# Feed-forward in steps of 512 hidden features, with block products of the next step between down products

## The chip, the cores and the metric

The kernel runs on one core of one Trainium2 chip. The metric is the device time in microseconds of one execution. The median of three runs of the kernel before is 1529.01 us (1528.41 to 1530.18). "The profile" is what the hardware profiler recorded in one execution; the engines are called PE (TensorE, matmuls), DVE (VectorE), ACT (ScalarE) and SP (SyncE, which issues the loads here).

## The reference

Two layers on a sequence of 16 + 512 positions of width 1024. Each has a token mixer and then a feed-forward part; only the latter is touched:

```python
def _sq_relu_mlp(h, w1, w2):
    return jnp.square(jax.nn.relu(h @ w1)) @ w2
...
        h = _layer_norm(DEEPNORM_ALPHA * h + _sq_relu_mlp(h, ffn_w1[layer], ffn_w2[layer]),
                        ln_g[layer, 1], ln_b[layer, 1])
```

`w1` is 1024 x 4096 and `w2` 4096 x 1024, in float32. Layer 0 works on all 528 positions (two halves of 264), layer 1 on the 512 that are returned (two halves of 256).

## The kernel before

**Precision.** Every operand of a product is split into a high part in the fast float32 format (an ACT cast, L228 for weights, which writes `wh`) and the remainder (a DVE subtraction, L229, which writes `wl`). A product runs three passes per 128 rows of the contraction: high by high, high by low, low by high. So the third matmul of a product is the first that needs `wl`.

**Weights.** `weight_plan` lists the weight tiles in the order of use. SP loads each into one of three `raw` buffers (`rpool`) of 128 x 1024 numbers. `weights(kind)` hands out the next item and prepares one or two items ahead. An item "A" is 1024 rows by 128 columns, an item "C" 512 rows by 256 columns, each one tile; an item "Q" is two tiles, for a block product. All split weights, activations and intermediates lie in 43 buffers of one pool (`upool`).

**Hidden features.** Feature tiles of 128: 32 of them in `ffn_w1`. The first eight are computed as plain products over K = 1024 (`job`, `squared`), six of them in `mlp_start`. The other 24 are computed two at a time as a **block product** (`quad_up`): the 1024 x 256 block of `w1` against both halves of the positions is formed with seven multiplications of half blocks in place of eight, in the manner of Strassen and Winograd. PE runs the seven in the order 11, a, b, 12, d, c, 22 (`multiply`), each 12 matmuls of half the positions. Their results go into the PSUM tiles `qa`, `qb`, `qc`, `qd`; the combinations are small DVE operations (L1167, L1169, L1174, L1176, L1180). 22 is left over (`finish`) and is run by `between` a little later; behind it come the squared ReLU (L1182), ACT's cast of g (L1183) and its remainder (L1184).

The weights of a block product need sums of blocks before they can be split. `quad_steps` is a generator, and each `advance()` runs one step of the next item that is not finished:

```python
        h, l = halves(r0)
...
        dve.tensor_tensor(out=s0.rearrange("p (a b) -> p a b", a=2), in0=r0.rearrange("p (a b) -> p a b", a=2),
                          in1=dup(r1[:, hi], 512), op=ALU.add)
...
        h, l = halves(s0)
        quad["c"], quad["a"] = (h[:, lo], l[:, lo]), (h[:, hi], l[:, hi])
...
        dve.tensor_tensor(out=s1[:, hi], in0=s1[:, lo], in1=r1[:, lo], op=ALU.add)
...
        h, l = halves(s1)
        quad["b"], quad["d"] = (h[:, lo], l[:, lo]), (h[:, hi], l[:, hi])
```

On DVE a preparation is thus L229 (first raw tile), L242 (first sums), L229 (first sums, for a and c), L248 and L250 (second sums), L253 (remainder of block 12), L229 (second sums, for b and d). ACT has the four casts.

**Down products.** The features of a group of eight tiles (`NG` = 4 groups) are multiplied with `w2`, one product over K = 1024 for each of the eight output tiles `y`; DVE adds each into `y` (L1096 the first time, L1094 later). In layer 0 such a product is 48 matmuls of 264 columns into `mm` (two PSUM buffers, shared with `qb` and `qd`), in layer 1 it is 24 matmuls of 512 columns into `bank` (four buffers, shared with `qa` and `qc`).

**The order.** Group 0's features, group 0's down products with two `advance()` behind each, then all four block products of group 1 and the first of group 2 in a row, group 1's down products, and so on. The last group goes to `tail`, which runs two products in full and the last six output tiles half by half, the layer norm between them. The compiler's scheduler puts the instructions of DVE, ACT and SP into an order of its own; with `pe.on` the order of the matmuls is held as written. Each engine then has a fixed list.

## Time and profile before

| | |
|---|---|
| median of three runs | 1529.01 us |
| the profiled execution | 1526.21 us |
| its span, first to last instruction | 1524.4 us |
| mean granted PE clock | 0.994 |
| DVE, additions of down products (L1094), layer 0 | 17 of 0.701 us, without the last group's half products |
| loads of raw tiles | 224 of 512 KB |

The span is the time from the first to the last instruction; the rest of the execution, 1.8 us, lies around it. "Busy" is the time in which an engine had an instruction running; matmuls overlap, so that one of 264 columns lasts 0.28 us but the next starts 0.12 us after it. Feed-forward 0 runs from about 345 to 725 us of the span, feed-forward 1 from about 1150 us to the end.

### The profile page before, as it was taken

Reading aid. Unit: us, or ns where it says so; the run is one execution under the profiler, and the core shown is the slowest. Engines: PE = TensorE matmul, PEld = TensorE weight load, DVE = VectorE, ACT = ScalarE, POOL = GpSimd, SP = SyncE. Lnnn points to the kernel's source line nnn. Section 1 sums busy time; section 2 is a strip of 40 time slices with the busy share of each in tenths; the row PEclk is TensorE's granted clock in tenths of the full one; section 3 lists DMA queues with packets and bytes.
Section 4 is the critical chain, followed back from the end, with each engine's and each line's share of the span. In section 5 each row is a group of like instructions: output and inputs, shape, how many; then the busy total and the mean of one; then the engine's idle time right before and its main releaser. Section 6 shows DMA issues by size and latency. Waiting matters only on the chain.

```text
span 1524.4 us, 23188 instructions
## 1 busy us (share of the span) xinstructions
PE 1485.1 (97%) x9752; PEld 1334.4 (88%) x9752; DVE 922.8 (61%) x1522; ACT 609.4 (40%) x972; POOL 0.2 (0%) x4
## 2 busy tenths in 40 slices
PE   8999999999999999999999999999999999999997
PEld 6887878799999999999888888888899888898986
DVE  4574466677758576568534354254477848676567
ACT  4474444536324233245343442153445524233323
POOL 0000000000000000000000000000000000000000
PEclk9999999999999999999999999999999999999999
DMA  6111102141313323243014035022150313313221
GB/s 243 51 48 55 56 29 85 57 138 32 97 55 91 116 70 125 71 132 117 28 42 137 14 109 166 0 89 90 56 168 27 111 56 97 124 62 133 83 70 56
DMA packets 39593, 129.02 MB, mean 85 GB/s; under 512 B 4725, under 2 KB 7173, under 8 KB 39489
## 3 DMA queue, kind: packets, MB, share of 16 engines
q1 hardware_dynamic: 39488, 127.54, 26.1%
q8 instruction: 76, 1.25, 0.3%
q14 instruction: 29, 0.23, 0.0%
HBM read 125.43 MB, written 2.10 MB: 84 GB/s over the span
## 4 chain that ended last, share of the span: by engine, by line
PE 86%; DVE 9%; ACT 2%; DMA 2%; issue 1%; ACTq 0%; DVEq 0%
PE bank L156 33%; PE mm L156 21%; PE v_ps L156 10%; PE qc L156 5%; PE o_ps L156 5%; PE s_ps L156 4%; DVE wl L229 3%; PE qa L156 3%; DMA raw<-in_w 2%; PE qd L156 2%; ACT wh L228 1%; PE t_ps L159 1%; PE qb L156 1%; PE sum_ps L156 1%; DVE up L1182 1%
## 5 line engine op out<-in xcount | busy, mean ns | idle before, releaser
L229 DVE TENSOR_TENSOR wl<-raw,wh 128x1024 fp32r<-128x1024 f32 x200 | 242.3, 1221 | 71.6 <-ACT wh L228 70.9
L228 ACT CAST wh<-raw 128x1024 fp32r<-128x1024 f32 x200 | 205.9, 1046 | 107.7 <-DMA raw<-in_w 75.8
L156 PE MATMUL bank<-g,wh 128*128 128x512 f32 (+2 forms) x800 | 202.3, 344 | 3.4 <-ACT g L1183 2.9
L156 PEld LDWEIGHTS bank<-g,wh 128*128 128x128 f32 x800 | 138.4, 190 | 22.0 <-ACT g L1183 3.1
L156 PE MATMUL bank<-hh,wh 128*128 128x512 f32 (+3 forms) x448 | 144.2, 337 | 0.0
L156 PE MATMUL bank<-hh,wl 128*128 128x512 f32 (+3 forms) x448 | 140.4, 330 | 0.0
L156 PE MATMUL mm<-g,wh 128*128 128x264 f32 x832 | 136.5, 286 | 2.5 <-ACT g L1183 2.0
L156 PE MATMUL bank<-g,wl 128*128 128x512 f32 (+2 forms) x400 | 136.5, 342 | 0.0
L156 PE MATMUL bank<-hl,wh 128*128 128x512 f32 (+3 forms) x448 | 120.8, 331 | 4.3 <-DVE hl L948 4.3
L156 PEld LDWEIGHTS mm<-g,wh 128*128 128x128 f32 x832 | 116.3, 190 | 2.9 <-ACT g L1183 2.2
L156 PE MATMUL qc<-tc,wh 128*128 128x264 f32 (+1 forms) x576 | 107.1, 284 | 2.0 <-ACT wh L228 1.8
L156 PEld LDWEIGHTS bank<-hh,wh 128*128 128x128 f32 x448 | 84.0, 188 | 10.7 <-ACT hh L960 1.2
L156 PE MATMUL mm<-s,wh 128*128 128x264 f32 x544 | 92.8, 292 | 0.5 <-DVE s L362 0.5
L156 PEld LDWEIGHTS qc<-tc,wh 128*128 128x128 f32 x576 | 89.0, 188 | 3.6 <-ACT wh L228 3.3
L156 PEld LDWEIGHTS bank<-hh,wl 128*128 128x128 f32 x448 | 83.9, 188 | 8.4
L156 PE MATMUL qc<-tc,wl 128*128 128x264 f32 (+1 forms) x288 | 82.5, 287 | 5.3 <-DVE wl L229 5.1
L156 PE MATMUL mm<-g,wl 128*128 128x264 f32 x416 | 85.0, 286 | 0.0
L156 PEld LDWEIGHTS bank<-hl,wh 128*128 128x128 f32 x448 | 72.6, 188 | 14.0 <-DVE hl L948 4.9
L156 PEld LDWEIGHTS bank<-g,wl 128*128 128x128 f32 x400 | 75.5, 189 | 9.3
L228 ACT CAST wh<-sums 128x1024 fp32r<-128x1024 f32 x48 | 50.4, 1049 | 76.8 <-DVE sums L242 32.5
L156 PEld LDWEIGHTS mm<-s,wh 128*128 128x128 f32 x544 | 74.9, 188 | 6.8 <-issue 2.3
L229 DVE TENSOR_TENSOR wl<-sums,wh 128x1024 fp32r<-128x1024 f32 x48 | 58.6, 1221 | 27.6 <-PE mm L156 10.3
(314 smaller groups left out, 3098.5 us busy)
## 6 DMA issues: line engine op xcount, KB each, us to landing
raw<-in_w SPq DMA_DIRECT2D x224, 512.0 KB, 4.1
xf<-in_x SPq DMA_DIRECT2D x8, 264.0 KB, 5.4
y<-in_x SPq DMA_DIRECT2D x8, 264.0 KB, 4.1
out<-y SPq DMA_DIRECT2D x8, 256.0 KB, 2.2
nb<-in_c_nb SPq DMA_DIRECT2D x4, 264.0 KB
rd<-in_c_rd SPq DMA_DIRECT2D x4, 256.0 KB
rd<-in_c_rm SPq DMA_DIRECT2D x4, 192.0 KB, 4.2
fm<-in_c_fm SPq DMA_DIRECT2D x1, 264.0 KB, 2.7
```

Source lines behind the costliest of these rows:

```text
L156: return self.put(nc.tensor.matmul(*a, **k))
L159: return self.put(nc.tensor.transpose(*a, **k))
L228: act.copy(out=wh, in_=raw)
L229: dve.tensor_tensor(out=wl, in0=raw, in1=f(wh), op=ALU.subtract)
L1182: dve.scalar_tensor_tensor(out=rs, in0=rs, scalar=0.0, in1=rs, op0=ALU.max, op1=ALU.mult)
```

## The change

The hidden features are taken in steps of 512 (four feature tiles, two block products) in place of groups of 1024. The down product of a step is over K = 512, with C tiles of `w2`: one C tile serves two output tiles. Steps 0 to 5 are handled so. Step 0's eight down products come first; then each step s from 1 to 5 runs a block product, two C tiles (four down products), a block product, two C tiles. The block products are those of step s + 1, one step ahead. Features 3072 to 4095 (the last two steps) still go through K = 1024 products with A tiles; their first two output tiles are run over the first six feature tiles each before the last two tiles are used. The combinations of activations for the block products (`combined`) are spread over step 0's down products.

```diff
-        for f in range(8):
-            up(0, f)
-        for g in range(NG):
-            if g and g + 1 < NG:
-                quad(g + 1, 0)
-            for f in range(KT):
-                down(g, f)
-            if g + 1 < NG:
-                for q in range(min(g, 1), 4):
-                    quad(g + 1, q)
+        def down(s, c):
+            plan.append(("C", "ffn_w2", layer, 512 * s, 256 * c))
 
         for f in range(8):
+            plan.append(("A", "ffn_w1", layer, 0, P * f))
+        for c in range(4):
+            down(0, c)
+        for s in range(1, 6):
+            for i in range(2):
+                quad(2 * s + 2 + i)
+                down(s, 2 * i)
+                down(s, 2 * i + 1)
+        quad(14)
+        quad(15)
+        for f in range(KT):
+            plan.append(("A", "ffn_w2", layer, 3072, P * f))
...
-            for _ in range(4):
+            for _ in range(2):
                 next(mix, None)
-        run_all(mix)
...
+        def down(s, c, hook):
+            wts = weights("C")
+            for j in range(2):
+                wt = tuple(p[:, :, P * j:P * j + P] for p in wts)
+                add_into(y[2 * c + j], None if s else ALPHA)(dense(wt, gs[4 * s:4 * s + 4], full), full)
                 between()
-                pe.on = False
-                return tail(jobs, full, a, b, norm, steps)
-            for k, (get, run) in enumerate(jobs):
-                run(get(), full)
-                if k == 0:
-                    between()
-                advance()
-                advance()
-            pe.on = True
-            gs = nxt
-            quads(gs, 4 - len(gs) // 2)
+                hook()
+
+        for c in range(4):
+            down(0, c, lambda: next(mix, None))
+        run_all(mix)
+        gs[:4] = [None] * 4
+        pe.on = True
+        for s in range(1, 6):
+            for i in range(2):
+                quad()
+                down(s, 2 * i, advance)
+                down(s, 2 * i + 1, advance)
+            gs[4 * s:4 * s + 4] = [None] * 4
+        quad()
+        quad()
+        between()
+        last = gs[24:]
+        parts = [dense_parts(weights("A"), last, full) for _ in range(2)]
+        for lo, hi in ((0, 6), (6, 8)):
+            for _, outs, pairs in parts:
+                product(outs, pairs, lo, hi)
```

What this makes of the engines' lists is shown at three places of layer 0. The line numbers of the helpers are the same in both kernels; `sums` are the block sums, `up` the pre-activations of a block product, `tv` its intermediates.

DVE, the preparation of a block product before the change, from the third y addition of a group with earlier block products:

```order
L1094 TENSOR_TENSOR y<-y,mm 128x528
L229 TENSOR_TENSOR wl<-raw,wh 128x1024
L242 TENSOR_TENSOR sums<-raw 128x1024
L1094 TENSOR_TENSOR y<-y,mm 128x528
L229 TENSOR_TENSOR wl<-sums,wh 128x1024
L248 TENSOR_TENSOR sums<-sums,raw 128x512
L1094 TENSOR_TENSOR y<-y,mm 128x528
L250 TENSOR_TENSOR sums<-sums,raw 128x512
L253 TENSOR_TENSOR w_5922<-raw,w_5922 128x512
L229 TENSOR_TENSOR wl<-sums,wh 128x1024
L1094 TENSOR_TENSOR y<-y,mm 128x528
```

and in the changed kernel, from the second of the four y additions between two block products to the next block product's first combination:

```order
L1094 TENSOR_TENSOR y<-y,mm 128x528
L1184 TENSOR_TENSOR g<-up,g 128x1056
L242 TENSOR_TENSOR sums<-raw 128x1024
L1094 TENSOR_TENSOR y<-y,mm 128x528
L229 TENSOR_TENSOR wl<-sums,wh 128x1024
L248 TENSOR_TENSOR sums<-sums,raw 128x512
L229 TENSOR_TENSOR wl<-raw,wh 128x1024
L1094 TENSOR_TENSOR y<-y,mm 128x528
L253 TENSOR_TENSOR w_4846<-raw,w_4846 128x512
L250 TENSOR_TENSOR sums<-sums,raw 128x512
L229 TENSOR_TENSOR wl<-sums,wh 128x1024
L1167 TENSOR_TENSOR tv<-qb,tv 128x264
```

The second sums' split stood ahead of three more y additions of full products; now it is the last thing ahead of the block product's own combinations, and a C tile's split stands in the middle of the preparation.

PE, the start of a block product: before the change most follow another block product directly (the end of multiply c, then the next product's 11):

```order
L156 MATMUL qc<-tc,wh 128x264 x2
L156 MATMUL qc<-tc,wl 128x264
L156 MATMUL qc<-tc,wh 128x264 x2
L156 MATMUL qc<-tc,wl 128x264
L156 MATMUL qa<-hh,wh 128x264
L156 MATMUL qa<-hl,wh 128x264
L156 MATMUL qa<-hh,wl 128x264
```

in the changed kernel eleven of twelve follow down products:

```order
L156 MATMUL mm<-g,wh 128x264 x4
L156 MATMUL mm<-g,wl 128x264 x2
L156 MATMUL mm<-g,wh 128x264 x4
L156 MATMUL mm<-g,wl 128x264 x2
L156 MATMUL qa<-hh,wh 128x264
L156 MATMUL qa<-hl,wh 128x264
L156 MATMUL qa<-hh,wl 128x264
```

The down products in front of it were four of 24 matmuls, with the former block product's 22 behind the first of them.

PE, the last block product of the layer: before, part of the last group's first product stood ahead of its multiply 22:

```order
L156 MATMUL mm<-g,wl 128x264 x2
L156 MATMUL mm<-g,wh 128x264 x4
L156 MATMUL qc<-tc,wh 128x264 x2
L156 MATMUL qc<-tc,wl 128x264
L156 MATMUL qc<-tc,wh 128x264 x2
L156 MATMUL qc<-tc,wl 128x264
```

now 22 follows multiply c at once, both into `qc` (16 rows in all, of which the piece shows the last four), and the down products come behind:

```order
L156 MATMUL qc<-tc,wh 128x264 x2
L156 MATMUL qc<-tc,wl 128x264
L156 MATMUL qc<-tc,wh 128x264 x2
L156 MATMUL qc<-tc,wl 128x264
L156 MATMUL mm<-g,wh 128x264 x4
L156 MATMUL mm<-g,wl 128x264 x2
```

The first product's matmuls on older features moved behind 22, and the feature tiles of the last block product are used only after both output tiles' first six pairs.

## The prediction

> **What bounds the kernel now.** First the page: how busy is each engine, and does TensorE ever rest?

> ```profile
> span 1524.4 us, 23188 instructions
> PE 1485.1 (97%) x9752; PEld 1334.4 (88%) x9752; DVE 922.8 (61%) x1522; ACT 609.4 (40%) x972; POOL 0.2 (0%) x4
> ```

> TensorE is busy 97% of the span, so only what it waits for, or how many matmuls it runs, can move the time. Next the view of TensorE's waits, whole program (what waits, for whom: us in total, times, longest):

> ```profile
> PE qc L156 <- DVE wl L229: 5.1, 7, 1.0
> PE bank L156 <- ACT g L1183: 2.9, 1, 2.9
> PE mm L156 <- ACT g L1183: 2.0, 1, 2.0
> PE qc L156 <- ACT wh L228: 1.8, 4, 0.7
> ```

> All four lie in the feed-forward: block products (qc) wait for split weights, and the last group's first product for the last g. What a matmul costs there is read from the chain of work (start, us, what):

> ```profile
> 381.69 56.58 PE mm L156 x465
> ...
> 1190.00 53.23 PE bank L156 x230
> 1243.23 1.41 PE qa L156 x12
> ```

> That is 0.1217 us for 264 columns, 0.2314 for 512, 0.1175 for 256. What the feed-forwards lose altogether comes from where they start and end (timeline: first down product; the third product of the last group, or the first sum behind it):

> ```profile
> 391.41 0.28 PE L156 MATMUL mm<-g,wh 128*128 128x264 f32 x1
> ...
> 675.99 0.28 PE L156 MATMUL bank<-g,wl 128*128 128x264 f32 x1
> ...
> 1198.63 0.63 PE L156 MATMUL bank<-g,wh 128*128 128x512 f32 x2
> ...
> 1482.57 0.59 PE L156 MATMUL sum_ps<-acc,ones 128*128 128x256 f32 x2
> ```

> Layer 0: three groups of 384 down matmuls, 12 block products of 84, two products of 48 and 2 strays are 2258, by 0.1217 = 274.8 us; it took 284.6: **9.8 lost**. Layer 1: 624 by 0.2314 + 1080 by 0.1175 = 271.3; it took 283.9: **12.6 lost**. The change can win at most 22.4 us.

> **The change, part by part.** Matmuls: 56 products of K = 512 or 1024 in place of 32 of K = 1024, the same count per layer. No gain and no cost there. DMA: again 4 raw tiles for one block product and two C tiles. New: 24 more additions into y per layer, and above all a new order on DVE, which now sits between four short down products and the next block product. So DVE is laid against TensorE. Durations on DVE in layer 0 (count | busy, mean ns):

> ```profile
> L229 DVE TENSOR_TENSOR wl<-sums,wh 128x1024 fp32r<-128x1024 f32 x24 | 29.3, 1221 | 13.8 <-PE mm L156 10.3 <-ACT wh L228 3.3
> L1184 DVE TENSOR_TENSOR g<-up,g 128x1056 fp32r<-128x1056 f32 x12 | 15.1, 1257 | 12.0 <-ACT g L1183 12.0
> L242 DVE TENSOR_TENSOR sums<-raw 128x1024 f32<-128x1024 f32 x12 | 14.6, 1220 | 0.8 <-DMA raw<-in_w 0.7
> L1094 DVE TENSOR_TENSOR y<-y,mm 128x528 f32<-128x528 f32 x17 | 11.9, 701 | 24.5 <-PE mm L156 24.5
> L250 DVE TENSOR_TENSOR sums<-sums,raw 128x512 f32<-128x512 f32 x12 | 8.2, 684 | 0.0
> ```

> and two that are shorter in layer 1:

> ```profile
> L1184 DVE TENSOR_TENSOR g<-up,g 128x1024 fp32r<-128x1024 f32 x12 | 14.7, 1224 | 11.7 <-ACT g L1183 11.7
> L1094 DVE TENSOR_TENSOR y<-y,bank 128x512 f32<-128x512 f32 x17 | 11.6, 684 | 22.5 <-PE bank L156 22.5
> ```

> Queued behind each other they start closer than they last; and the handover DVE, ACT, DVE, TensorE at the end of a preparation stands once in the trace, as a stall (timelines of DVE, ACT, TensorE):

> ```profile
> 565.58 1.25 DVE L1182 SCALAR_TENSOR_TENSOR up<-up 128x1056 f32<-128x1056 f32 x1
> 566.75 1.22 DVE L229 TENSOR_TENSOR wl<-sums,wh 128x1024 fp32r<-128x1024 f32 x1
> 567.89 0.68 DVE L248 TENSOR_TENSOR sums<-sums,raw 128x512 f32<-128x512 f32 x1
> 568.49 0.68 DVE L253 TENSOR_TENSOR w<-raw,w 128x512 fp32r<-128x512 f32 x1
> 569.09 1.25 DVE L1184 TENSOR_TENSOR g<-up,g 128x1056 fp32r<-128x1056 f32 x1
> 570.26 0.68 DVE L250 TENSOR_TENSOR sums<-sums,raw 128x512 f32<-128x512 f32 x1
> 572.06 1.22 DVE L229 TENSOR_TENSOR wl<-sums,wh 128x1024 fp32r<-128x1024 f32 x1 [1.12 <-ACT wh L228]
> ...
> 570.98 1.05 ACT L228 CAST wh<-sums 128x1024 fp32r<-128x1024 f32 x1 [2.95 <-DVE sums L250]
> ...
> 572.08 0.51 PE L156 MATMUL qc<-tc,wh 128*128 128x264 f32 x2
> 573.34 0.39 PE L156 MATMUL qc<-tc,wl 128*128 128x264 f32 x1 [0.75 <-DVE wl L229]
> ```

> Steps: L1182 1.17, wl 1.14, L248, L250 and L253 0.60, L1184 1.17, each 0.08 under its duration; so L242 1.14 and y 0.62. Handover: 0.04 from L250 to ACT, 1.05 there, 0.03 to wl, 1.22, 0.05 to the matmul. TensorE runs two matmuls on wh and stops at the third for wl. A y addition starts 0.21 after the next product's start:

> ```profile
> 497.08 0.29 PE L156 MATMUL qc<-tc,wh 128*128 128x264 f32 x1
> ...
> 497.29 0.70 DVE L1094 TENSOR_TENSOR y<-y,mm 128x528 f32<-128x528 f32 x1 [3.13 <-PE mm L156]
> ```

> Now the steady period of the new order, layer 0, from T = 0, where the third of the four down products starts (a down product: 24 x 0.1217 = 2.92; a multiply of a block product: 12 x 0.1217 = 1.46). DVE starts: second y 0.21; g (L1184) 0.83; L242 2.00; third y 3.14; then wl of the first sums, held by ACT's cast (L242 ends 3.22, cast 3.26 to 4.31), 4.33; L248 5.47; wl of the next C tile 6.07; fourth y, which TensorE would allow at 6.05, 7.21; behind it in the queue L253 7.83; L250 8.43 to 9.11; cast 9.15 to 10.20; wl of the second sums 10.23 to 11.45. TensorE: down products to 5.84, multiply 11 to 7.30, a to 8.76, and now b, which needs the second sums: it starts at 10.25 in place of 8.76, stops at 10.49, goes on at 11.50. **Stall 1.49 + 1.01 = 2.5 us.** All that sets it starts at TensorE's second down product, and DVE has idle time again behind b, so it neither grows nor heals: it comes back every period. In layer 1 (down product 2.78, multiply 1.41, y 0.68, L1184 1.22) the same walk gives L1184 0.82, third y 3.10, wl 4.29, L248 5.43, fourth y 6.03, wl C 6.64, L253 7.78, L250 8.38, wl to 11.40, while b could start at 8.38: **1.82 + 1.00 = 2.8 us**.

> How often: block product 1 of a layer was prepared between eight products of step 0 (its second wl stands before the last y): no stall. Numbers 2 to 10: nine each, 22.5 + 25.2. Number 11 has no C tile ahead, so L253 comes at 6.07 and L250 at 7.29: 1.4 and 1.7. Number 12 directly follows 11: 0 and 0.3. At the end 22 follows c at once and waits for L1176 (0.21 + 0.42 + 0.05 = 0.7), and the second A tile's wl stands behind the last g: about 0.6; both layers 2.6. The sum is **53.7 added**. The old losses (22.4) go: block products no longer follow each other, and the last g is needed only after 72 matmuls on older g (8.8 us). **Net +31.**

> Hidden, and why: a tile's load

> ```profile
> raw<-in_w SPq DMA_DIRECT2D x224, 512.0 KB, 4.1
> ```

> Three raw buffers rotate. The last of a period's loads that matter, the second raw tile, waits for L250 and is used by L242 one period later, some 17 us after: room for three loads of 4.1 in a row. SP's order puts no load behind one that waits longer. ACT's casts stand ahead of their use in the same walk. If that cover went, each period would lose up to one load, 4.1 us.

> What the trace of before does not show is a stall every 24 us. Does the clock hold? Windows of 3.41 us around one of the longest waits, and one that held (first PE busy, then the other engines; PEclk stands behind POOL):

> ```profile
> 663.62:667.03 3.41, 0.98 (x6) 0.55 (x5) 2.20 (x2) 2.05 (x3) 0.00 (x0) 1.00 0.00 0
> 667.03:670.45 3.42, 3.40 (x15) 3.40 (x16) 3.42 (x4) 1.87 (x2) 0.00 (x0) 0.50 0.21 37
> 1284.84:1288.25 3.41, 1.95 (x15) 1.54 (x13) 2.23 (x2) 3.31 (x5) 0.00 (x0) 1.00 0.63 190
> ```

> After a window with 2.4 us idle the clock was 0.50 for 3.41 us, which costs 1.7; after one with 1.5 us idle it held. The new pair of waits leaves about 2.1 (layer 0) or 2.4 us idle by the same reckoning (0.16 less for each, a matmul's tail), if one window holds it whole. Bounds: none of 18, or all 18 (31 us). With windows that fall anywhere, a quarter to a half of the periods: I take five, 8.5 us, nearer to the row with 2.4.

> [...]

> **The rivals.** (1) No half clock: +31, so 1557 on the profiled execution, 1560 beside the median. (2) On the other side, DVE keeps up: the fine mixing gives preparation enough room, b never waits, only the end's 2.6 are paid: -20, 1509. It decides when the second sums' wl is through 2.5 us sooner, for instance with L250 ahead of wl of the C tile and the fourth y. For it: DVE's work in a period, five wl (5.7), L242 (1.1), L248, L250 and L253 (1.8), four y (2.5), L1182 and L1184 (2.3) and five short ones

> ```profile
> 1258.55 0.34 DVE up L1180
> ```

> (1.7) make 15 us of 22. Against: the rows from 565.58 on run without a gap, so it takes one thing after the other, and 9.4 of the 15 us, with 1.7 of waiting for ACT, stand from the second y to the second sums' wl, a stretch that TensorE passes in 8.6. (3) The clock drops in more than half the periods, or a load comes late now and then: +31 and 17 to 30, 1578 to 1590. (4) Waits and savings cancel: the stall would have to be 1.1 us per period, which no step of the walk allows; a chance of 0.02.

> **How the numbers follow.** The profiled execution took 1526.2 (span 1524.4 and 1.8 around it); the median of the runs shown is 1529.0, 2.8 above. 1526.2 + 31 + 8.5 = 1566, and 1568 beside the median with most of that 2.8. Chances: this forecast 0.60 (1562 to 1578), (1) 0.20, (3) 0.12, (2) 0.06, (4) 0.02. Range 1554 to 1582: the stalls at 2.2 us each without half clock, up to ten half-clock windows and 0.3 us more per stall. 0.2% is about what a measurement of this kernel can tell from no change: slower 0.92, same 0.02, faster 0.06.

> **What will show it.** TensorE's waits: qc for ACT's wh (L228), about 20 times, some 27 us, and qc for DVE's wl (L229), 20 times about 0.75; the waits for ACT's g gone. In the timeline, DVE busy from the second y to L250 but for half a microsecond, and periods of 24.4 and 23.8 us in place of 21.9 (180 x 0.1217) and 21.0 (84 x 0.1175 + 48 x 0.2314). Windows with PEclk 0.50 behind some stalls. Wrong if y additions or wl start earlier than the walk says, or if b finds its weights ready.

## The result, and the profile after

The changed kernel is slower: **1573.38 us** median of four runs (1569.08 to 1582.64), beside 1528.71 us for the kernel before in the same comparison (1525.95 to 1530.18). The ratio is **1.0298**, 95% interval 1.0262 to 1.0333. The profiled execution took 1573.18 us, span 1571.4, mean granted clock 0.987; that of before took 1526.21, span 1524.4, so 47.0 us are to be explained.

The page of the changed kernel, span and busy time:

```profile
span 1571.4 us, 23263 instructions
PE 1499.3 (95%) x9752; PEld 1344.2 (86%) x9752; DVE 956.0 (61%) x1570; ACT 608.6 (39%) x972; POOL 0.2 (0%) x4
```

The matmuls are as many as before, DVE has its 48 more additions. TensorE is busy 14 us longer, though it does the same work, and the rest of the 47 us is time in which it was idle. Its waits (us in total, times, longest), the four that matter in the feed-forward:

```profile
PE qc L156 <- ACT wh L228: 28.4, 20, 1.7
PE qc L156 <- DVE wl L229: 15.1, 20, 0.8
...
PE sum_ps L156 <- DVE acc L913: 2.0, 1, 2.0
...
PE qc L156 <- DVE up L1176: 1.2, 2, 0.6
```

Both waits for ACT's g are gone, and twenty block products wait twice each: first for ACT's `wh`, then for DVE's `wl`. One period in the timelines, DVE from the second y addition to the second sums' split, then ACT's cast, then TensorE at multiply b:

```profile
454.07 0.70 DVE L1094 TENSOR_TENSOR y<-y,mm 128x528 f32<-128x528 f32 x1 [1.19 <-PE mm L156]
454.69 1.25 DVE L1184 TENSOR_TENSOR g<-up,g 128x1056 fp32r<-128x1056 f32 x1
455.86 1.22 DVE L242 TENSOR_TENSOR sums<-raw 128x1024 f32<-128x1024 f32 x1
457.00 0.70 DVE L1094 TENSOR_TENSOR y<-y,mm 128x528 f32<-128x528 f32 x1
458.26 1.22 DVE L229 TENSOR_TENSOR wl<-sums,wh 128x1024 fp32r<-128x1024 f32 x1 [0.56 <-ACT wh L228]
459.40 0.68 DVE L248 TENSOR_TENSOR sums<-sums,raw 128x512 f32<-128x512 f32 x1
460.00 1.22 DVE L229 TENSOR_TENSOR wl<-raw,wh 128x1024 fp32r<-128x1024 f32 x1
461.14 0.70 DVE L1094 TENSOR_TENSOR y<-y,mm 128x528 f32<-128x528 f32 x1
461.75 0.68 DVE L253 TENSOR_TENSOR w<-raw,w 128x512 fp32r<-128x512 f32 x1
462.36 0.68 DVE L250 TENSOR_TENSOR sums<-sums,raw 128x512 f32<-128x512 f32 x1
464.15 1.23 DVE L229 TENSOR_TENSOR wl<-sums,wh 128x1024 fp32r<-128x1024 f32 x1 [1.11 <-ACT wh L228]
...
463.07 1.05 ACT L228 CAST wh<-sums 128x1024 fp32r<-128x1024 f32 x1 [3.38 <-DVE sums L250]
...
464.17 0.51 PE L156 MATMUL qc<-tc,wh 128*128 128x264 f32 x2 [1.40 <-ACT wh L228]
465.43 0.39 PE L156 MATMUL qc<-tc,wl 128*128 128x264 f32 x1 [0.76 <-DVE wl L229]
```

The order is that of the walk in the prediction, and so are the times: from the second y to the second sums' split it said 10.02 us (0.21 to 10.23), and 10.08 passed (454.07 to 464.15).

Then the clock. Windows of 3.41 us, one stall whose window lies badly, one that held (PEclk stands behind POOL):

```profile
463.01:466.43 3.42, 1.50 (x10) 1.30 (x11) 1.60 (x3) 1.32 (x2) 0.00 (x0) 1.00 0.80 303
466.43:469.84 3.41, 3.41 (x17) 3.41 (x17) 0.43 (x1) 0.00 (x0) 0.00 (x0) 0.50 0.02 7
1319.79:1323.20 3.41, 2.11 (x15) 1.90 (x16) 1.67 (x3) 0.77 (x2) 0.00 (x0) 1.00 0.78 300
1323.20:1326.61 3.41, 3.41 (x31) 3.41 (x30) 1.05 (x2) 2.10 (x3) 0.00 (x0) 1.00 0.02 5
```

In the half-clock window TensorE is busy throughout, but the row counts 17 matmuls, where the last one, at full clock, has 31. Seven of these lie behind block products (from 439.1, 466.4, 541.5, 616.6, 1272.0, 1418.7 and 1442.6), and an eighth, from 719.0, lies behind TensorE's wait for the layer norm's sum (`sum_ps`) at the end of layer 0. Before there were two in the feed-forwards.

Where the 47 us lie is read from the first and the last matmul on g in each layer: before, from 391.41 and 1198.63 (shown with the prediction) to

```profile
712.95 0.28 PE L156 MATMUL bank<-g,wl 128*128 128x264 f32 x1
...
1510.45 0.28 PE L156 MATMUL bank<-g,wl 128*128 128x256 f32 x1
```

and in the changed kernel

```profile
388.56 0.40 PE L156 MATMUL mm<-g,wh 128*128 128x264 f32 x2
...
735.42 0.28 PE L156 MATMUL bank<-g,wl 128*128 128x264 f32 x1
...
1223.05 0.40 PE L156 MATMUL bank<-g,wh 128*128 128x512 f32 x1
...
1557.45 0.27 PE L156 MATMUL bank<-g,wl 128*128 128x256 f32 x1
```

So 321.5 and 311.8 us became 346.9 and 334.4: +25.3 and +22.6. Everything else together gives -0.9. The sum of these two stretches is called "feed-forward" below: 633.4 us before, 681.3 after.

### The profile page after: what moved, and what is told of

Same layout as the page of the kernel before. It is cut to its first block, busy times and chain, and to the rows that moved or that the text cites. A ratio compares the mean times of both kernels' runs of the same rounds, so it can differ in the third digit from the quotient of the medians.

```text
span 1571.4 us, 23263 instructions
## 1 busy us (share of the span) xinstructions
PE 1499.3 (95%) x9752; PEld 1344.2 (86%) x9752; DVE 956.0 (61%) x1570; ACT 608.6 (39%) x972; POOL 0.2 (0%) x4
## 3 DMA queue, kind: packets, MB, share of 16 engines
q1 hardware_dynamic: 39488, 127.54, 25.3%
q8 instruction: 76, 1.25, 0.3%
## 4 chain that ended last, share of the span: by engine, by line
PE 79%; DVE 14%; ACT 4%; issue 1%; DMA 1%; ACTq 0%; DVEq 0%
PE bank L156 30%; PE mm L156 15%; PE v_ps L156 10%; PE qc L156 7%; PE o_ps L156 4%; PE s_ps L156 4%; DVE wl L229 4%; ACT wh L228 3%; PE qa L156 3%; PE qd L156 2%; DVE y L1094 2%; DVE g L1184 2%; DVE sums L242 1%; DMA raw<-in_w 1%; PE t_ps L159 1%
## 5 line engine op out<-in xcount | busy, mean ns | idle before, releaser
L229 DVE TENSOR_TENSOR wl<-raw,wh 128x1024 fp32r<-128x1024 f32 x200 | 241.7, 1220 | 83.9 <-ACT wh L228 83.4
L228 ACT CAST wh<-raw 128x1024 fp32r<-128x1024 f32 x200 | 205.3, 1047 | 75.2 <-DMA raw<-in_w 66.2
L156 PE MATMUL bank<-g,wh 128*128 128x512 f32 (+2 forms) x800 | 202.3, 344 | 0.2 <-ACT wh L228 0.2
L156 PEld LDWEIGHTS bank<-g,wh 128*128 128x128 f32 x800 | 137.4, 190 | 17.5 <-ACT wh L228 1.0
L156 PE MATMUL bank<-hh,wh 128*128 128x512 f32 (+3 forms) x448 | 145.6, 340 | 0.0
L156 PE MATMUL bank<-hh,wl 128*128 128x512 f32 (+3 forms) x448 | 141.2, 332 | 0.0
L156 PE MATMUL qc<-tc,wh 128*128 128x264 f32 (+1 forms) x576 | 112.6, 292 | 29.5 <-ACT wh L228 28.4
L156 PE MATMUL bank<-g,wl 128*128 128x512 f32 (+2 forms) x400 | 136.7, 342 | 0.0
L156 PE MATMUL mm<-g,wh 128*128 128x264 f32 x832 | 134.8, 284 | 0.0
L156 PE MATMUL bank<-hl,wh 128*128 128x512 f32 (+3 forms) x448 | 120.8, 332 | 4.2 <-DVE hl L948 4.2
L156 PEld LDWEIGHTS qc<-tc,wh 128*128 128x128 f32 x576 | 91.8, 193 | 34.9 <-ACT wh L228 32.5
L156 PEld LDWEIGHTS mm<-g,wh 128*128 128x128 f32 x832 | 115.0, 188 | 0.0
L228 ACT CAST wh<-sums 128x1024 fp32r<-128x1024 f32 x48 | 50.4, 1050 | 152.0 <-DVE sums L250 79.3
L156 PE MATMUL qc<-tc,wl 128*128 128x264 f32 (+1 forms) x288 | 85.9, 298 | 15.1 <-DVE wl L229 15.1
L156 PEld LDWEIGHTS bank<-hh,wh 128*128 128x128 f32 x448 | 85.0, 190 | 10.6 <-ACT hh L960 1.2
L156 PE MATMUL mm<-s,wh 128*128 128x264 f32 x544 | 92.8, 292 | 0.5 <-DVE s L362 0.5
L156 PEld LDWEIGHTS bank<-hh,wl 128*128 128x128 f32 x448 | 84.8, 190 | 8.6
L1183 ACT CAST g<-up 128x1056 fp32r<-128x1056 f32 (+1 forms) x24 | 25.5, 1064 | 153.2 <-DVE up L1182 153.2
L156 PEld LDWEIGHTS bank<-hl,wh 128*128 128x128 f32 x448 | 72.8, 189 | 14.0 <-DVE hl L948 4.9
L156 PE MATMUL mm<-g,wl 128*128 128x264 f32 x416 | 84.5, 284 | 0.0
L156 PEld LDWEIGHTS bank<-g,wl 128*128 128x128 f32 x400 | 75.9, 190 | 9.3 <-DVE wl L229 0.2
L229 DVE TENSOR_TENSOR wl<-sums,wh 128x1024 fp32r<-128x1024 f32 x48 | 58.8, 1226 | 37.5 <-ACT wh L228 37.5
## 6 DMA issues: line engine op xcount, KB each, us to landing
raw<-in_w SPq DMA_DIRECT2D x224, 512.0 KB, 4.2
```

Source lines behind the costliest of these rows:

```text
L156: return self.put(nc.tensor.matmul(*a, **k))
L228: act.copy(out=wh, in_=raw)
L229: dve.tensor_tensor(out=wl, in0=raw, in1=f(wh), op=ALU.subtract)
L1183: act.copy(out=hs_, in_=rs)
```

## The experiments

**Theory A:** each block product waits at multiply b because the last step of its preparation stands too late in DVE's queue, and the longer rests then bring half-clock windows. **Rivals:** the wait has another cause (a load, ACT's own queue, DVE's work as a whole), or the half clock comes from elsewhere. Each run is timed beside the kernel before on the same chip, and the ratios are to that. The chip was not the same for all, but the medians of the kernel before lie within 0.3% of each other: 1528.71 us for the changed kernel; 1530.15 for "advance twice", "prepared three ahead", "before, new end of layer" and "idle matmuls, first wait"; 1530.3 for "L248 twice, idle matmuls" and "before, two ahead"; 1532.4 for the other four.

| kernel | median us (range) | ratio to before, interval | feed-forward us | half-clock windows in it |
|---|---|---|---|---|
| before | 1528.71 (1525.95 to 1530.18) | 1 | 633.4 | 2 |
| after | 1573.38 (1569.08 to 1582.64) | 1.0298 (1.0262 to 1.0333) | 681.3 | 8 |
| advance twice | 1564.59 (1559.60 to 1566.67) | 1.0229 (1.0199 to 1.0259) | 666.1 | 5 |
| prepared three ahead | 1514.19 (1512.97 to 1514.80) | 0.9909 (0.9888 to 0.9930) | 615.8 | 0 |
| the same, last one late | 1510.85 (1509.51 to 1512.49) | 0.9872 (0.9843 to 0.9901) | 611.0 | 0 |
| before, new end of layer | 1523.82 (1518.08 to 1526.03) | 0.9952 (0.9934 to 0.9970) | 626.2 | 0 |
| idle matmuls, first wait | 1567.09 (1559.65 to 1575.12) | 1.0257 (1.0207 to 1.0307) | 668.6 | 0 |
| idle matmuls, both waits | 1565.13 (1558.34 to 1568.11) | 1.0220 (1.0181 to 1.0259) | 668.3 | 0 |
| L248 twice | 1618.34 (1613.84 to 1619.84) | 1.0569 (1.0534 to 1.0603) | 718.8 | 26 |
| L248 twice, idle matmuls | 1584.92 (1582.44 to 1585.81) | 1.0359 (1.0317 to 1.0401) | 685.9 | 2 |
| L1174 three times | 1575.22 (1573.13 to 1577.99) | 1.0297 (1.0259 to 1.0336) | 673.7 | 3 |
| before, two ahead | 1544.82 (1538.29 to 1551.27) | 1.0100 (1.0054 to 1.0146) | 647.6 | 1 |

The last two columns are of the profiled execution.

### Prepared three items ahead

```diff
-        while queue["next"] < min(len(plan), queue["used"] + 1 + (1 if kind == "Q" else ahead)):
+        while queue["next"] < min(len(plan), queue["used"] + 1 + (3 if kind == "Q" else ahead)):
```

When a block product begins, the next one is already in the list, so its preparation runs between the multiplies, where DVE had idle time, and ahead of the four y additions.

> Theory A (place): the loss is the preparation of the next block product, which stands on DVE behind the y additions of the last four down products. Here the next block product's tiles are taken three items ahead, so that its preparation is run between the multiplies of the block product before. On DVE the second sums' split then stands ahead of the first of the four y additions, some 10 us before it is used. A: the waits of qc for wh and wl are gone (below 5 us in all), so 50 us of stall and most half-clock windows go: 1573 - 50 - 12 = about 1510. Theory B (work): 24 more additions per layer and products of K = 512 cost by themselves; then the time stays above the kernel before, 1529 or more. Theory C: two preparations at once do not fit the 43 buffers, and waits of DVE and ACT for PE take the place of the old ones: 1530 to 1570.

Measured: 1514.19 us, the waits at b gone. What TensorE still waits for in the feed-forward:

```profile
PE qa L156 <- ACT tv L1165: 2.6, 2, 1.5
...
PE qc L156 <- DVE tv L1169: 1.0, 2, 0.6
PE qc L156 <- DVE up L1176: 0.6, 1, 0.6
```

DVE has the same operations as in the changed kernel and is busy as long (958.3 us). So it is their place, not their amount, that costs 59 us of 1573 (65.5 us within the feed-forward; outside it this execution had more half-clock windows than that of the changed kernel, see the end). The new order of the products is not the loss; the preparation that was hung on it is.

### Two steps of preparation behind each down product

```diff
-                down(s, 2 * i, advance)
-                down(s, 2 * i + 1, advance)
+                down(s, 2 * i, twice)
+                down(s, 2 * i + 1, twice)
```

where `twice` calls `advance` two times.

> Two steps of the preparation behind each down product in place of one. On DVE this moves only the C tile's split from the middle of the preparation to behind it. A, by the walk: L253 and L250 come 1.14 us earlier, the wait at b falls from 2.5 to 1.4 us in layer 0 and from 2.8 to 1.7 in layer 1, 18 times: -20 us, and with only 1.0 to 1.3 us idle in one place hardly any half-clock window behind a block product, another -8 to -12: 1541 to 1546. B (work on DVE, not its place): no change, 1573.

Measured: 1564.59, a miss of some 20 us with the step itself right. TensorE's waits:

```profile
PE qc L156 <- DVE wl L229: 15.1, 20, 0.8
PE qa L156 <- ACT tv L1165: 12.7, 2, 6.4
PE qc L156 <- ACT wh L228: 8.3, 20, 0.7
```

The wait for wh fell from 28.4 to 8.3 us as walked, but the eleventh block product of each layer now waits 6.4 us for ACT's copy of `qa`. ACT's timeline in front of it:

```profile
656.65 1.04 ACT L228 CAST wh<-raw 128x1024 fp32r<-128x1024 f32 x1
660.36 1.04 ACT L228 CAST wh<-sums 128x1024 fp32r<-128x1024 f32 x1 [2.67 <-DVE sums L242]
661.31 0.61 ACT L252 CAST w<-raw 128x512 fp32r<-128x512 f32 x1
664.50 1.04 ACT L228 CAST wh<-sums 128x1024 fp32r<-128x1024 f32 x1 [2.58 <-DVE sums L250]
665.45 0.37 ACT L1165 COPY tv<-qa 128x264 f32<-128x264 f32 x1
```

These casts are those of the twelfth block product; ACT takes them in order, each waits for DVE, and the copy of 0.37 us, which has to be done before the multiply named 12 may write into `qa`, stands behind all of them. Twice the steps mean that the last preparation too is drawn in at once. The five half-clock windows of this run lie behind these two waits (two from 663.2, three from 1478.9) and none behind the waits at b, which is what A said of them. The time outside the feed-forward was 8.7 us longer than in the changed kernel's profile, and that makes part of the miss.

### The new end of the layer alone, in the kernel before

The last group's first two output tiles over the first six feature tiles, then over the last two, in the old order; nothing else.

```diff
+                parts = [dense_parts(weights("A"), gs, full) for _ in range(2)]
+                for lo, hi in ((0, 6), (6, 8)):
+                    for _, outs, pairs in parts:
+                        product(outs, pairs, lo, hi)
...
-                return tail(jobs, full, a, b, norm, steps)
+                return tail(jobs[2:], full, a, b, norm, steps)
```

> The kernel before with one part of the change alone: at the end of each layer the first two output tiles run over the first six feature tiles each before the last two. Theory: the wait for the last g (5 us by the profile, with the half-clock window behind each, about 8 in all with matmuls at half speed) goes, and the new order pays the wait of 22 for L1176 (0.6 each) and perhaps 0.6 for the second tile's split: 1529 - 8 + 2 = 1521 to 1524. Rival: the time at the end of a layer is set by the loads and the layer norm, not by PE: no change, 1529.

Measured over ten runs: 0.9952 (0.9934 to 0.9970), 1523.82 us. The waits for the last g (2.9 and 2.0 us) are gone, the feed-forward is 7.2 us shorter, of which two half-clock windows are 3.3. This part of the change is a gain by itself.

### Idle matmuls in the waits

```diff
+        for k in range(fill):
+            pe.matmul(pc, lhsT=quad["11"][0][:, P * (k % 4):P * (k % 4) + P], rhs=plain(0, c1)[k % 4][0], start=True, stop=True)
         multiply(pc, "b", mixed(1), True)
```

with `fill` 11 in block products 2 to 10.

> Block products 2 to 10 of each layer run 11 additional matmuls of one multiply's kind (1.3 us) between multiplies a and b, into the buffer that b then overwrites. They lie in the time in which PE waits for wh of the second sums. If the half clock is set off by these waits, as theory A has it: the wait for wl stays (about 0.75 each), the start of b stays where it is, but PEclk is 1.00 behind all block products; the seven half-clock windows there (1.7 us each) go: about 1561, with less spread between executions. If the half clock has another cause: windows stay, 1573. If PE was not really free there: up to 18 x 1.3 = 24 us more.

Measured: the median is 1567.09, but the four runs fall apart: 1562.03 and 1559.65 at a clock of 0.996, 1572.14 and 1575.12 at 0.989 and 0.988. In the profiled one, of the first kind, no half-clock window is left behind the block products. To see whether the slower ones come from the second wait, that one was filled too, with eight matmuls ahead of the third of multiply b:

```diff
+                    for j in range(extra if k == 0 and i == 2 else 0):
+                        pe.matmul(pd, lhsT=quad["11"][0][:, P * (j % 4):P * (j % 4) + P], rhs=plain(0, c1)[j % 4][0], start=True, stop=True)
                     pe.matmul(ps, lhsT=wt[p][:, P * k:P * k + P], rhs=xs[k][q], start=first and k == 0 and i == 0, skip_group_check=not first,
```

> The changed kernel with idle matmuls in both waits of block products 2 to 10: eleven ahead of multiply b (as in the run before) and eight between its second and third matmul, results unused, so that TensorE has no long idle time there while b comes as late as before. Theory A (half-clock windows come from the idle time of the two waits together): none is left inside the feed-forwards, and all runs lie at 1556 to 1562 with a clock of 0.994 or more. Theory B (the runs of 1572 to 1575 with the first filler alone have their half clock from elsewhere, the token mixers or the layer norms): the runs spread as before, 1560 to 1575.

Measured: 1565.13, runs at 1558.34 to 1568.11 with clocks of 0.997 to 0.991; between the two theories. In the feed-forward the answer is plain: no window at half clock, and 668.3 us in place of 681.3. That is 13.0 less with the stalls as long as before (from the last matmul of multiply a to the third of b, the 24 block products took 61.5 us in all, and 60.8 in the changed kernel). It fits what the matmuls of the changed kernel lost in its eight windows, read from the distances of their starts: 12.3 us, about 1.5 each. The three windows left in that execution's span before its last matmuls lie in the token mixer (see the end). Where the slower runs lose theirs wasn't traced.

### One DVE operation more, inside the stretch and outside

L248 (0.60 us) computed twice, so that one operation more stands ahead of the second sums' split:

```diff
         dve.tensor_tensor(out=s1[:, lo], in0=s0[:, hi], in1=r0[:, lo], op=ALU.add)
+        dve.tensor_tensor(out=s1[:, lo], in0=s0[:, hi], in1=r0[:, lo], op=ALU.add)
```

> The changed kernel with the first half of the second sums (L248) computed twice, so that one more DVE operation of 0.60 us stands in the queue ahead of the second sums' split in each block product. Theory A (each block product waits at multiply b for exactly the work that DVE's queue holds from the second y addition on): TensorE's wait for ACT's wh at b grows by 0.60 us in each of some 20 block products, +12 us, and half-clock windows may add a few us: 1583 to 1592; the wait qc for ACT wh goes from 28.4 to about 40 us, the wait for DVE wl stays 15.1. Theory B (b waits for something else, a load or ACT's own queue): the added operation disappears in DVE's idle time and the time stays at 1573.

L1174 computed three times, two operations more where DVE is idle behind b:

```diff
         dve.tensor_tensor(out=r[:, 0, two_], in0=pd, in1=m, op=ALU.subtract)
+        dve.tensor_tensor(out=r[:, 0, two_], in0=pd, in1=m, op=ALU.subtract)
+        dve.tensor_tensor(out=r[:, 0, two_], in0=pd, in1=m, op=ALU.subtract)
```

> The changed kernel with the difference L1174 computed three times, so that two more DVE operations, together 0.68 us, stand in each block product, but behind multiply b, where DVE has idle time ahead of the first y addition. Theory A (only the stretch from the second y addition to the second sums' split counts): no change, 1569 to 1580, and TensorE's waits at b stay 28.4 and 15.1 us. Theory B (DVE's total work in a period decides): as with the operation inside the stretch, +13 us, 1585 or more.

The same 16 us more of busy DVE in both (972.0 and 971.8 against 956.0). Outside the stretch: 1575.22 us, no change, and the two waits for wh and wl read

```profile
PE qc L156 <- ACT wh L228: 28.3, 20, 1.7
PE qc L156 <- DVE wl L229: 15.1, 20, 0.8
```

Inside: 1618.34, and

```profile
PE qc L156 <- ACT wh L228: 42.9, 20, 2.5
```

The wait grew by 14.5 us, 0.72 for each block product. (Not 0.60, because L250 reads the repeated result and starts 0.71 behind it.) So a queue that is idle 39% of the span sets the time, by what stands in one stretch of it. But 45 us were lost, not 14.5, and both theories missed that; 37.5 of them lie in the feed-forward. The windows of layer 1 show why:

```profile
1338.90:1342.31 3.41, 1.28 (x11) 1.08 (x10) 2.46 (x4) 0.82 (x1) 0.00 (x0) 1.00 0.53 151
1342.31:1345.72 3.41, 2.67 (x11) 2.38 (x12) 1.56 (x2) 0.49 (x2) 0.00 (x0) 0.51 0.86 298
1345.72:1349.14 3.42, 3.42 (x18) 3.42 (x18) 0.43 (x1) 0.20 (x1) 0.00 (x0) 0.50 0.03 12
1349.14:1352.55 3.41, 3.41 (x27) 3.29 (x27) 2.25 (x3) 2.07 (x3) 0.00 (x0) 1.00 0.03 8
```

Two windows in a row at half clock, and this behind block product after block product: 26 such windows in the two feed-forwards. If they are the cause, filling the waits must take the excess away and leave the 14.5. The next kernel has L248 twice and both fillers, the first with sixteen matmuls:

```diff
-                quad(11 if (s, i) != (1, 0) else 0)
+                quad(16 if (s, i) != (1, 0) else 0)
```

> The kernel with L248 computed twice, which took 1618 us where 1585 was expected, and with idle matmuls in both waits of block products 2 to 10 (sixteen ahead of multiply b, eight between its second and third matmul; results unused), so that the stalls stay as long but TensorE rests little in them. Theory A (the added operation costs 14.5 us of longer stalls, the other 30 us are half-clock windows that the longer rests bring on): the windows in the feed-forwards go, and 1566 to 1580 is left, some 14 us above the changed kernel with the same kind of filler. Theory B (the added operation delays something else as well): 1595 or more, at a clock of 0.99.

Measured: 1584.92 us. That is 5 us over A's range, but the feed-forward settles it: 685.9 us with two half-clock windows, against 668.3 with the same kind of filler and L248 once. Of these 17.6 us the two windows are 3.0, which leaves 14.6 for the longer stalls (14.5 by the waits). The filler takes 718.8 to 685.9, and nearly all of these 32.9 us were half clock: the matmuls in the 26 windows had lost 37.5 us, those in the two that are left lose 3.0. What A had not counted are these 3.0 us and 3.2 outside the feed-forward, where this execution had six half-clock windows against three.

### Is early preparation the whole gain?

The kernel before, with one item more prepared ahead at a block product:

```diff
-        while queue["next"] < min(len(plan), queue["used"] + 1 + (1 if kind == "Q" else ahead)):
+        while queue["next"] < min(len(plan), queue["used"] + 1 + (2 if kind == "Q" else ahead)):
```

> The kernel before, with one item more prepared ahead at a block product (two in place of one; three fit only the order of the change, since here block products follow each other and share the three raw buffers). Theory A (the old order has its waits because block products in a row leave DVE too little time, so that earlier preparation alone gains little): 1522 to 1536, waits of qc for wh and wl between 4 and 9 us. Theory B (preparing earlier is the whole gain, and the change's order adds nothing to it): those waits fall under 2 us and the time to 1518 to 1523, with the waits for the last g kept.

Measured: 1544.82, slower by 1.0%, outside both ranges. The waits for wh and wl are gone, and TensorE waits for the small combinations:

```profile
PE qc L156 <- DVE tv L1169: 13.7, 10, 1.8
PE qa L156 <- ACT tv L1165: 8.3, 6, 1.9
...
PE qc L156 <- DVE up L1176: 5.2, 6, 1.2
```

In the old order four block products follow each other. What is put earlier there goes ahead of the combinations of a running block product, on DVE and on ACT. So the earlier preparation did not pay in the old order; it paid in the new one, in which down products lie between block products.

### The version that beats both

Three items ahead, but the twelfth block product, which directly follows the eleventh, only one:

```diff
-        while queue["next"] < min(len(plan), queue["used"] + 1 + (1 if kind == "Q" else ahead)):
+        while queue["next"] < min(len(plan), queue["used"] + 1 + (ahead if kind != "Q" else 1 if plan[queue["used"] + 1][0] == "Q" else 3)):
```

> The kernel that prepares a block product during the one before it (three items ahead), but with the item after the eleventh block product prepared only one ahead, so that the casts of the twelfth no longer stand ahead of the eleventh's copy of qa (L1165) in ACT's queue. In the former version TensorE lost 1.2 and 0.6 us there in layer 0, and 1.7, 0.7 and 0.8 us in layer 1. Theory A (that queue order is the cause): these 5 us go, 1508 to 1511. Theory B (the twelfth's split is then late at its own multiply b, as in the changed kernel): the wait moves there, 1512 to 1516.

Measured: **1510.85 us**, 0.9872 (0.9843 to 0.9901) of before; theory A. The waits at L1165 and L1169 are gone. The feed-forward is 22.4 us shorter than in the kernel before (611.0 against 633.4), the figure that the prediction had set as the most that this change could win. That the two agree to the tenth is chance, since the prediction read its figure from shorter stretches.

## Why the prediction was right, and where it was off

It said 1568 (1554 to 1582) and slower; 1573.4 was measured, with the slowest of the four runs at 1582.6. Point by point, in us of the profiled execution. The measured column sums the distances between starts of matmuls, less the spacing of unhindered ones, and keeps what falls in half-clock windows apart.

| step | predicted | measured |
|---|---|---|
| stalls at multiply b and at the layer's end | +53.7 | +51.8 |
| half clock behind them | +8.5 (five windows) | +10.6 (seven) |
| losses of before that go | -22.4 | -19.2 |
| in the feed-forward: wait for the layer norm's sum, the half-clock window behind it, wider spacing | 0 | +4.7 |
| outside the feed-forward | 0 | -0.9 |
| sum | +39.8 | +47.0 |

- **The stalls.** At b in layer 0 nine by 2.5 were 22.5, measured 22.0; in layer 1 nine by 2.8 were 25.2, measured 24.9. The eleventh: 1.4 and 1.7, measured 1.4 and 1.6. The twelfth cost 0 and 0.2, where 0 and 0.3 were said, and the second A tile, where 0.6 a layer was said, 0.2 us once. The walk along the queue held because each duration came from rows of the same operation, and because the order of the queue was known.
- **The cause.** That it is the stretch from the second y to the second sums' split, and neither DVE's load nor a transfer, is shown from three sides: the same work outside the stretch costs nothing, an operation inside it lengthens the wait by what its spacing says, and the preparation moved out of it takes the waits away.
- **The half clock** was mis-sized, by two windows that were missing, and a little by the price. It was taken as half of 3.41 us, 1.7 for each. But in a half-clock window a matmul of 264 columns starts 0.22 us behind the one before it (as from 719.24 to 719.46), in place of 0.1217, so a window full of them loses 3.41 x (1 - 0.1217/0.22) = 1.5. The prediction had one row that dropped (0.98 busy) and one that held (1.95), and took "a quarter to a half of the periods", then five. In the profile after, half clock followed windows with 1.17 to 1.75 us busy and, within the feed-forwards, none with 1.87 or more, so nearer to the row that held. No wait at b was longer than 1.7 us in one piece, yet half clock followed seven of the twenty stalls in this execution, and three in one of the others with stalls as long (L1174 three times). The count thus did not come from the length of the stalls alone, and that five came as near as it did is in part luck. That half clock was rightly in the sum is shown by the filled waits.
- **The old losses.** 22.4 were taken as all to go. 15.9 of them were waits that went, 3.3 were two half-clock windows, and the rest, matmuls a little farther apart than reckoned, stayed. Behind the stretch that the prediction looked at, the wait for the layer norm's sum in layer 0 grew (from start to start 2.25 us at 718.35, in place of 1.41), and a half-clock window of 1.7 us followed it. The prediction had neither in its sum.
- **The rivals.** That DVE keeps up (1509) would need the second sums' split 2.5 us sooner; the runs with the preparation moved reach that time, 1510.85, so the price was right and the condition was not met. Without half clock (1560): the filled waits give 1558.3 to 1562.0 in the executions with a clock of 0.996 or more.

## What to carry to other kernels

When an engine's queue is fixed, lay it out in time against the engine that waits for it: utilization (DVE 61%) did not show the loss here; the queue between the last event it must wait for and the result that is needed did. When work is cut finer and interleaved, move its preparation by the same amount, and check the first and the last item of the chain, which follow another rule. Repeated short rests of TensorE cost more here than their length: with L248 twice the waits for wh grew by 14.5 us in all and the time by 45 us, though no rest at b lasted longer than 2.5 us in one piece.

## What the runs showed of the hardware

**Stalls eight windows apart.** With L248 twice, a period of layer 1 at full clock would by estimate be about 24.7 us (24.0 in the changed kernel from 1344.27 to 1368.23, between two starts of multiply b with no half clock, and 0.7 more). The starts of multiply b:

```profile
1369.66 0.80 PE L156 MATMUL qc<-tc,wh 128*128 128x256 f32 x2 [2.40 <-ACT wh L228]
...
1396.85 0.72 PE L156 MATMUL qc<-tc,wh 128*128 128x256 f32 x2 [2.44 <-ACT wh L228]
...
1424.06 0.63 PE L156 MATMUL qc<-tc,wh 128*128 128x256 f32 x2 [2.45 <-ACT wh L228]
...
1451.36 0.64 PE L156 MATMUL qc<-tc,wh 128*128 128x256 f32 x2 [2.39 <-ACT wh L228]
...
1478.68 0.65 PE L156 MATMUL qc<-tc,wh 128*128 128x256 f32 x2 [2.45 <-ACT wh L228]
```

lie 27.2 to 27.3 us apart, which is eight windows of 3.413 (27.30). The page of this run has PEclk between 0.8 and 0.9 in the four slices from 1332 to 1494 us; two half-clock windows in each 27.3 us would give 0.875. Whether the half clock itself holds the period at that length was not shown, since no run moved the stalls against the windows. What is measured is that a stall of 0.7 us more went with 26 windows in place of eight, and with a mean granted clock of 0.965 in place of 0.987.

**Half clock without rest.** In the token mixer some executions have stretches at half clock behind windows in which TensorE was busy throughout, as here in the fastest kernel (two windows at clocks of 1.00 and 0.50, and a part of TensorE's timeline in the first of them):

```profile
162.60:166.00 3.40, 3.40 (x26) 3.14 (x24) 1.93 (x2) 1.81 (x3) 0.00 (x0) 1.00 0.00 0
166.00:169.40 3.40, 3.40 (x14) 3.11 (x15) 1.56 (x4) 1.59 (x5) 0.00 (x0) 0.50 0.50 154
...
164.03 0.96 PE L156 MATMUL o_ps<-s 16*128 16x512 f32 x3
164.83 1.50 PE L156 MATMUL mo_ps<-s 16*128 16x16 f32 x12
```

The matmuls shown in the first window have only 16 rows. Whether that is the cause wasn't tried and stays open: after has the same matmuls from 164.12 and 164.93, before has them from 166.93 and 167.73, and from 160 to 180 us both have a clock of 1.00 with TensorE 19.82 and 20.00 us busy. "Before, two ahead" has 0.66 there, 20.00 us busy. By the mean granted clocks, less the windows of the table, nine traces have 5 to 9 windows' worth of half clock outside the feed-forward, and the three others (before, after, and idle matmuls in the first wait) 3 to 4. The nine show 893.7 to 898.8 us there and the three 890.1 to 891.6, so part of the spread between runs goes with it.
